# A hybrid attention layer on one core: loads a step earlier in the second half's preparation, the mask inside the scan, one small product on ScalarE

## The chip, the core and the metric

The kernel runs on one core of a Trainium2 chip. A core has TensorE (PE; its weight loads are listed apart as PEld), VectorE (DVE), ScalarE (ACT), GpSimd (POOL) and SyncE (SP), which in this kernel issues the transfers between HBM and the core's memory. Each engine takes its instructions in the order in which the program holds them for it; between engines they wait on semaphores. The metric is the device time of one execution in microseconds (us), the median of several.

## What is computed

One mixer layer with batch 1, sequence 2048 and width 1024, in float32:

```python
mod = c @ w_ada + b_ada
shift, scale, gate = split(mod, 3)
h = rmsnorm(x, norm_g) * (1 + scale) + shift
sb_q, sb_k, sb_v, sb_g, df_q, df_k, df_v, df_g = split(h @ w_in)
# group A, 8 heads of 64, stick-breaking, strictly causal (s < t):
#   A[t, s] = sigmoid(z_ts) * prod over s < j < t of (1 - sigmoid(z_tj))
# group B, 4 heads, two softmax maps of 64 and values of 128, ALiBi, causal
sb_out = stick_breaking(sb_q, sb_k, sb_v) * silu(sb_g)
df_out = rmsnorm(p1 @ v - lam * p2 @ v) * 0.8 * silu(df_g)
out = concat(sb_out, df_out) @ w_out
return x + gate * out
```

## The kernel before

The sequence is worked on in two halves of 1024 rows, each in two chunks of 512 columns. Matrix products keep near-float32 accuracy by splitting an operand into a rounded part and a rest (`wh` and `wl`, `hH` and `hL`, `aH` and `aL`) and adding three products (`mm3`, lines 381 to 383).

**Start (lines 1013 to 1026).** For each of the eight 128-row blocks of the width, DVE reduces two tiles of `w_ada` against `c` (`ada_block`, L179, two instructions of 512 columns for the scale and two for the shift). Then `gmul` = (1 + scale) times the norm's gain is made on DVE (L1015, a 128x1 instruction), ACT scales and shifts the transposed input with it (L310) and rounds it (L311), POOL or DVE forms the rest (L312), and PE runs twelve products.

**The second half's preparation (`prep_steps`, `ada_steps`).** The normalised input of the second half is made in small steps which are woven among the projections and the attention of the first half. For each chunk there are eight steps `one` that load a 128x512 block of `x`, square it on ACT (L220, L223) and add it on POOL (L224); one step that turns the sums into a factor; and eight steps `three` that load the block again (L253), scale it on DVE (L244) and on ACT (L335) and store it to HBM (L336). Then sixteen steps load a tile of `w_ada` (L198) and reduce it on DVE (L199) for the gate. Each step issues its load and uses it in the same step. The tiles come from a pool of eight buffers (`stage`), which the projections' outputs use too.

**Stick-breaking heads (`SBHead.front`).** A row block of 128 queries is cut into pieces of at most 512 columns, the rightmost piece first. Two matmuls per piece make the scores (L547). In the piece that holds the diagonal, a third matmul adds a 128x128 mask of -1e30 above and on the diagonal (L550, 128 in all: 8 heads with 16 row blocks each). ACT makes sigmoid(z) into `s` (L680) and sigmoid(-z) in place (L681); DVE runs a scan from right to left that multiplies sigmoid(-z) up into `u` (L684); POOL multiplies `s` by the shifted `u` (L688). In the rightmost piece the scan starts from 1.0:

```python
ps = scores(q, self.kch, i, c0, we, dg if 0 <= dg < w else None)
nc.scalar.activation(s[:, c0:c0 + w], ps[:, :w], AF.Sigmoid, scale=0.125)
nc.scalar.activation(ps[:, :w], ps[:, :w], AF.Sigmoid, scale=-0.125)
top = c0 + w == L
nc.vector.tensor_tensor_scan(out=u[:, c0:c0 + w][:, ::-1], data0=ur, data1=dist[:, :w],
                             initial=1.0 if top else u[:, c0 + w:c0 + w + 1],
                             op0=ALU.mult, op1=ALU.bypass)
```

`s` and `u` lie in a pool of six large buffers. Later PE transposes `s` (L583), ACT and DVE split it (L589, L590) and PE multiplies it with the values (L665, L666).

**What sets the order.** A planner lists attention steps and projection steps with costs and interleaves the two lists so that projections are done when a head needs them. A projection or preparation step may be issued only after an attention matmul some way back (`issue_after`). The framework then orders each engine's instructions by its own estimate of when they can run, so an edit in one place can move instructions elsewhere.

Of the kernel before, what the change touches and what calls it, by code (L numbers as in the profile page):

```python
# [8 lines left out]
F32R = mybir.dt.float32r  # L9
# [18 lines left out]
MASKED = -1e30  # L28
# [9 lines left out]
PREP0, PREP1 = -90, -90  # L38
POOL_H = (1, 2, 3, 4, 5, 6)
# [7 lines left out]
def build(ctx: ExitStack, tc, xT, xN, cT, cK, normg, w_adaT, b_ada, w_in, qg, kg, lam4, subg, w_out,  # L47
# [47 lines left out]
    dist = ctile([128, T], "dist")  # L95
    maskr = ctile([128, 128], "maskr", F32R)
# [6 lines left out]
    def more_constants():  # L103
# [6 lines left out]
        for h in range(NDF):  # L110
# [9 lines left out]
        mk = tmp0[:, 384:512]  # L120
        nc.gpsimd.memset(mk, 0.0)
        nc.gpsimd.affine_select(out=mk, in_=mk, pattern=[[-1, 128]], compare_op=ALU.is_gt,
                                fill=MASKED, base=0, channel_multiplier=1)
        nc.gpsimd.tensor_copy(maskr, mk)
# [58 lines left out]
    def ada_steps(third):  # L183
        st = {}

        def first():
            st["cb"] = [stage("cb") for _ in range(2)]
            for i in range(2):
                nc.sync.dma_start(st["cb"][i], cT[i * 512:i * 512 + 512].unsqueeze(0)
                                  .broadcast_to([128, 512]))  # L190

        def step(j, i):
            if i == 0:
                st["s"] = col.tile([128, 2], F32, name="adas", tag="adas", bufs=1)
            s = st["s"]
            r0 = third * 1024 + j * 128
            wt = stage("wada2")
            nc.sync.dma_start(wt, w_adaT[r0:r0 + 128, i * 512:i * 512 + 512])  # L198
# [119 lines left out]
    def prep_steps(ch):  # L318
        st = {}

        def one(k):
            xt = load_x(1, ch, k, stage("xt"))
            if k == 0:
                st["acc"] = stage("xacc")
            sq_add(st["acc"], k, xt)
# [4 lines left out]
        def three(k):  # L330
            if k == 0:
                st["rb"] = spread(st["y"])
            xt = load_x(1, ch, k, stage("xt"))
# [3 lines left out]
        return ([lambda k=k: one(k) for k in range(KT)] + [two, lambda: None, lambda: None]  # L337
# [205 lines left out]
    def scores(q, kch, i, k0, w, diag=None):  # L543
        ps = zps.tile([128, 512], F32, name="ps_z", tag="z")
        tl = slice((i % 2) * 128, (i % 2) * 128 + 128)
        for pt in range(2):
            last_pe[0] = nc.tensor.matmul(ps[:, :w], lhsT=q[:, pt, tl], rhs=kch[k0 // 512][:, :w],  # L547
                                          start=pt == 0, stop=pt == 1 and diag is None)
        if diag is not None:
            last_pe[0] = nc.tensor.matmul(ps[:, diag:diag + 128], lhsT=identr, rhs=maskr, start=False,  # L550
                                          stop=True)
# [95 lines left out]
    class SBHead(Head):  # L647
# [20 lines left out]
        def front(self, i, A):  # L668
# [3 lines left out]
            def step(c0, w, we, first):  # L672
# [5 lines left out]
                dg = i * 128 - c0  # L678
                ps = scores(q, self.kch, i, c0, we, dg if 0 <= dg < w else None)
                nc.scalar.activation(s[:, c0:c0 + w], ps[:, :w], AF.Sigmoid, scale=0.125)  # L680
                nc.scalar.activation(ps[:, :w], ps[:, :w], AF.Sigmoid, scale=-0.125)  # L681
                top = c0 + w == L
                ur = ps[:, :w][:, ::-1]
                nc.vector.tensor_tensor_scan(out=u[:, c0:c0 + w][:, ::-1], data0=ur, data1=dist[:, :w],  # L684
# [606 lines left out]
```

## Time and profile before

| what | value |
|---|---|
| time, median of 3 runs | 1735.38 us (1733.97 to 1741.11) |
| time of the profiled execution | 1733.63 us |
| its span, first to last instruction | 1731.8 us |
| busy: PE, PEld, DVE, ACT, POOL | 1669.4, 1494.2, 1236.3, 1000.3, 836.6 us |
| share of the span | 96%, 86%, 71%, 58%, 48% |
| PE matmuls | 10816 |
| moved by DMA | 268.15 MB, mean 155 GB/s |

Busy time counts an instruction from its start to its end; since matmuls are pipelined, one begins before the one ahead of it ends, and a busy PE need not be a PE at its peak. What one matmul really takes of PE's time is read from start to start.

### The profile page before, as it was taken

The page shows a single profiled execution, that of the slowest core. Times are in us where ns is not written, and L with a number is a line of the kernel's source. Part 1 is how long each engine was busy: PE and PEld are TensorE (multiplying, and loading weights), DVE is VectorE, ACT ScalarE, POOL GpSimd, SP SyncE. Part 2 cuts the span into 40 slices and gives each one's busy share as a digit, 9 for nine tenths or more (in the row PEclk, how much of TensorE's full clock was granted, in tenths as well). Part 3 has the DMA queues.
Part 4 walks back from the last instruction along what each step waited for, and adds up shares of the span by engine and source line. Part 5 has one row for each costly group of instructions (what it writes and reads, how often), then busy time and mean ns, then how long its engine had stood idle before and what let it go on. Part 6 is the DMA issues. An engine that isn't in the chain of part 4 may idle for free.

```text
span 1731.8 us, 31619 instructions
## 1 busy us (share of the span) xinstructions
PE 1669.4 (96%) x10816; PEld 1494.2 (86%) x10816; DVE 1236.3 (71%) x2556; ACT 1000.3 (58%) x2027; POOL 836.6 (48%) x1266
## 2 busy tenths in 40 slices
PE   7899899999999999999999999999999999999999
PEld 6688688899999889878898889899998978888887
DVE  6626455766566887767787887788788889888741
ACT  4625555456555454766776777687665645554521
POOL 3325455457545644655565465576332353223553
PEclk9999999999999999999999999999999999999999
DMA  9585767534654975434432332234433566443264
GB/s 348 167 236 162 199 201 240 184 108 117 200 169 142 286 211 163 149 107 117 128 116 89 102 98 86 80 104 126 132 99 108 164 208 200 128 134 129 88 220 149
DMA packets 212690, 268.15 MB, mean 155 GB/s; under 512 B 21424, under 2 KB 136368, under 8 KB 212400
## 3 DMA queue, kind: packets, MB, share of 16 engines
q1 hardware_dynamic: 212528, 266.12, 50.5%
q8 instruction: 86, 1.41, 0.3%
q14 instruction: 76, 0.62, 0.1%
HBM read 186.34 MB, written 79.69 MB: 154 GB/s over the span
## 4 chain that ended last, share of the span: by engine, by line
PE 64%; DVE 8%; DMA 4%; issue 4%; POOL 3%; ACT 3%; SPq 1%; DVEq 0%; ACTq 0%; POOLq 0%
PE ps_z L547 10%; PE ps_t L583 8%; PE ps_n L381 5%; PE ps_n L383 5%; PE ps_n L382 5%; PE ps_p L381 4%; PE ps_p L383 4%; PE ps_p L382 4%; PE av L666 3%; PE av L665 3%; PE ps_o L381 3%; PE ps_o L382 3%; PE ps_o L383 3%; DMA xt<-in_xT 2%; DVE u L684 1%
## 5 line engine op out<-in xcount | busy, mean ns | idle before, releaser
L688 POOL TENSOR_TENSOR s<-s,u 128x512 f32<-128x512 f32 (+4 forms) x320 | 306.2, 959 | 274.1 <-DVE u L684 238.5
L547 PE MATMUL ps_z<-kc,qc 128*128 128x512 f32 (+3 forms) x1280 | 358.8, 374 | 10.5 <-DVE u L684 7.9
L589 ACT CAST aH<-ps_t 128x512 fp32r<-128x512 f32 (+1 forms) x432 | 240.7, 567 | 168.7 <-PE ps_t L583 165.1
L590 DVE TENSOR_TENSOR aL<-ps_t,aH 128x512 fp32r<-128x512 f32 (+1 forms) x432 | 276.7, 650 | 79.7 <-ACT aH L589 78.3
L369 POOL TENSOR_TENSOR wl<-raw,wh 128x512 fp32r<-128x512 f32 x168 | 224.5, 1344 | 128.1 <-ACT wh L365 118.3
L381 PE MATMUL ps_n<-wh,hH 128*128 128x256 f32 x960 | 275.2, 287 | 2.5 <-DVE sl L392 2.2
L383 PE MATMUL ps_n<-wh,hL 128*128 128x256 f32 x960 | 271.6, 283 | 0.0
L382 PE MATMUL ps_n<-wl,hH 128*128 128x256 f32 x960 | 271.2, 283 | 0.4 <-POOL wl L369 0.4
L684 DVE TENSOR_TENSOR_SCAN u<-ps_z,u,dist 128x512 f32<-128x512 f32 x192 | 245.7, 1280 | 32.2 <-ACT ps_z L681 26.5
L780 ACT ACTIVATE e<-e,nm 128x1024 f32<-128x1024 f32 (+4 forms) x192 | 172.1, 898 | 125.3 <-DVE nm L778 121.0
L547 PEld LDWEIGHTS ps_z<-kc,qc 128*128 128x128 f32 x1280 | 210.8, 190 | 37.4 <-DVE u L684 13.4
L766 DVE CUSTOM_DVE_ANT_0 e<-ps_z,dist 128x512 f32<-128x512 f32 (+3 forms) x320 | 186.6, 604 | 50.8 <-PE ps_z L547 44.0
L680 ACT ACTIVATE s<-ps_z 128x512 f32<-128x512 f32 (+3 forms) x320 | 172.9, 540 | 77.4 <-PE ps_z L547 39.2
L381 PE MATMUL ps_p<-hH,wh 128*128 128x512 f32 x480 | 192.2, 406 | 6.1 <-ACT hH L311 6.1
L382 PE MATMUL ps_p<-hL,wh 128*128 128x512 f32 x480 | 190.5, 397 | 0.8 <-POOL hL L312 0.6
L383 PE MATMUL ps_p<-hH,wl 128*128 128x512 f32 x480 | 189.3, 394 | 0.0
L381 PEld LDWEIGHTS ps_n<-wh,hH 128*128 128x128 f32 x960 | 182.6, 191 | 7.0 <-DVE sl L392 2.5
L382 PEld LDWEIGHTS ps_n<-wl,hH 128*128 128x128 f32 x960 | 182.7, 191 | 3.7 <-POOL wl L369 0.6
L383 PEld LDWEIGHTS ps_n<-wh,hL 128*128 128x128 f32 x960 | 182.8, 191 | 1.8
L681 ACT ACTIVATE ps_z<-ps_z 128x512 f32<-128x512 f32 (+3 forms) x320 | 173.5, 542 | 0.0
L583 PE MATMUL ps_t<-ident,s 128*128 128x128 f32 x1088 | 168.6, 275 | 4.6 <-DVE aL L590 4.3
L665 PE MATMUL av<-aH,vc 128*128 128x256 f32 x576 | 160.7, 290 | 7.9 <-ACT aH L589 6.7
(190 smaller groups left out, 3456.0 us busy)
## 6 DMA issues: line engine op xcount, KB each, us to landing
qc<-qst SPq DMA_DIRECT2D x256, 128.0 KB, 3.1
raw<-in_w_in SPq DMA_DIRECT2D x120, 256.0 KB, 3.2
kc<-kst SPq DMA_DIRECT2D x96, 256.0 KB, 3.5
vc<-vst SPq DMA_DIRECT2D x48, 256.0 KB, 3.0
vc<-vdt SPq DMA_DIRECT2D x48, 256.0 KB, 3.6
raw<-in_w_out SPq DMA_DIRECT2D x48, 256.0 KB, 3.4
wada<-in_w_adaT SPq DMA_DIRECT2D x16, 512.0 KB, 8.3
qst<-sh SPq DMA_DIRECT2D x64, 128.0 KB, 2.5
```

What stands on the lines that cost most here:

```text
L369: (eng or nc.gpsimd).tensor_tensor(out=wl, in0=raw, in1=wh.bitcast(F32), op=ALU.subtract)
L381: nc.tensor.matmul(ps, lhsT=aH, rhs=bH, start=first, stop=False)
L382: nc.tensor.matmul(ps, lhsT=aH, rhs=bL, start=False, stop=False)
L383: nc.tensor.matmul(ps, lhsT=aL, rhs=bH, start=False, stop=last)
L547: last_pe[0] = nc.tensor.matmul(ps[:, :w], lhsT=q[:, pt, tl], rhs=kch[k0 // 512][:, :w], start=pt == 0, stop=pt == 1 and diag is None)
L583: nc.tensor.transpose(tp[:, pos * 256 + t * 128:pos * 256 + t * 128 + 128], A[t][0][:, sb * 128:sb * 128 + 128], ident)
L589: nc.scalar.copy(aH[:, f0:], tp[:, f0:])
L590: nc.vector.tensor_tensor(out=aL[:, f0:], in0=tp[:, f0:], in1=aH[:, f0:].bitcast(F32), op=ALU.subtract)
L665: nc.tensor.matmul(o, lhsT=v, rhs=aH, start=st, stop=False)
L684: nc.vector.tensor_tensor_scan(out=u[:, c0:c0 + w][:, ::-1], data0=ur, data1=dist[:, :w], initial=1.0 if top else u[:, c0 + w:c0 + w + 1], ...
L688: nc.gpsimd.tensor_tensor(out=s[:, c0:c0 + m], in0=s[:, c0:c0 + m], in1=u[:, c0 + 1:c0 + m + 1], op=ALU.mult)
L766: nc.vector.tensor_tensor_reduce(out=e[m][:, c0 + o:c0 + o + w], in0=ps[:, :w], in1=dist[:, d0:d0 + w], scale=1.0, scalar=-3e38, op0=ALU.a ...
```

## The change

Four edits.

- **Preload.** In `prep_steps` and `ada_steps` the load of a block is issued in the step before the one that uses it (`PRELOAD = 1`), and each phase gets a step of its own that issues its first load (57 steps in the place of 55).
- **Mask in the scan.** The mask matmul, the mask and its making on POOL are gone. The table `dist`, which is loaded once at the start, gets 128 more columns with a one on the diagonal. In the rightmost piece the scan starts from 0.0 and its second operation is a maximum against that table: right of the diagonal it stays 0, on it it becomes 1. In the other pieces it is as it was.
- **Last column.** In that piece ACT writes one column less of `s`, and POOL writes the last one with a memset of 128x1 (128 in all).
- **`gmul` on ACT.** The eight 128x1 products of the start are now ACT instructions (gain times scale plus gain).

```diff
@@ -92,8 +92,9 @@
-    dist = ctile([128, T], "dist")
-    maskr = ctile([128, 128], "maskr", F32R)
+    dist = ctile([128, T + 128], "dist")
...
@@ -117,11 +118,6 @@
-        mk = tmp0[:, 384:512]
-        nc.gpsimd.memset(mk, 0.0)
-        nc.gpsimd.affine_select(out=mk, in_=mk, pattern=[[-1, 128]], compare_op=ALU.is_gt,
-                                fill=MASKED, base=0, channel_multiplier=1)
-        nc.gpsimd.tensor_copy(maskr, mk)
@@ -188,14 +184,22 @@
             for i in range(2):
                 nc.sync.dma_start(st["cb"][i], cT[i * 512:i * 512 + 512].unsqueeze(0)
                                   .broadcast_to([128, 512]))
+            for n in range(PRELOAD):
+                ld(n)
+
+        def ld(n):
+            if n < 2 * KT:
+                j, i = n // 2, n % 2
+                r0 = third * 1024 + j * 128
+                wt = st[(j, i)] = stage("wada2")
+                nc.sync.dma_start(wt, w_adaT[r0:r0 + 128, i * 512:i * 512 + 512])
 
         def step(j, i):
+            ld(2 * j + i + PRELOAD)
             if i == 0:
                 st["s"] = col.tile([128, 2], F32, name="adas", tag="adas", bufs=1)
             s = st["s"]
-            r0 = third * 1024 + j * 128
-            wt = stage("wada2")
-            nc.sync.dma_start(wt, w_adaT[r0:r0 + 128, i * 512:i * 512 + 512])
+            wt = st.pop((j, i))
             nc.vector.tensor_tensor_reduce(out=wt, in0=wt, in1=st["cb"][i], scale=1.0, scalar=0.0,
                                            op0=ALU.mult, op1=ALU.add, accum_out=s[:, i:i + 1])
             if i == 1:
@@ -318,11 +322,16 @@
     def prep_steps(ch):
         st = {}
 
+        def ld(n):
+            if n < 2 * KT:
+                st[n] = load_x(1, ch, n % KT, stage("xt"))
+
         def one(k):
-            xt = load_x(1, ch, k, stage("xt"))
+            if k + PRELOAD < KT:
+                ld(k + PRELOAD)
             if k == 0:
                 st["acc"] = stage("xacc")
-            sq_add(st["acc"], k, xt)
+            sq_add(st["acc"], k, st.pop(k))
 
         def two():
             st["y"] = row_rstd(st["acc"])
@@ -330,11 +339,13 @@
         def three(k):
             if k == 0:
                 st["rb"] = spread(st["y"])
-            xt = load_x(1, ch, k, stage("xt"))
+            ld(KT + k + PRELOAD)
+            xt = st.pop(KT + k)
             scale_x(xt, k, st["rb"])
             nc.scalar.activation(xt, xt, AF.Identity, bias=mod[:, k:k + 1])
             nc.sync.dma_start(hst[k][ch], xt)
-        return ([lambda k=k: one(k) for k in range(KT)] + [two, lambda: None, lambda: None]
+        return ([lambda: [ld(n) for n in range(PRELOAD)]] + [lambda k=k: one(k) for k in range(KT)]
+                + [two, lambda: None, lambda: [ld(KT + n) for n in range(PRELOAD)]]
                 + [lambda k=k: three(k) for k in range(KT)])
 
     def fetch_steps(ch, hH, hL):
@@ -540,15 +551,12 @@
                               src[u % 2, :, :, qs:qs + 256].rearrange("l p t -> p l t"))
         return qt
 
-    def scores(q, kch, i, k0, w, diag=None):
+    def scores(q, kch, i, k0, w):
         ps = zps.tile([128, 512], F32, name="ps_z", tag="z")
         tl = slice((i % 2) * 128, (i % 2) * 128 + 128)
         for pt in range(2):
             last_pe[0] = nc.tensor.matmul(ps[:, :w], lhsT=q[:, pt, tl], rhs=kch[k0 // 512][:, :w],
-                                          start=pt == 0, stop=pt == 1 and diag is None)
-        if diag is not None:
-            last_pe[0] = nc.tensor.matmul(ps[:, diag:diag + 128], lhsT=identr, rhs=maskr, start=False,
-                                          stop=True)
+                                          start=pt == 0, stop=pt == 1)
         return ps
 
     def segs(n, ext):
@@ -675,16 +683,19 @@
                 if first:
                     tiles["u"], tiles["s"] = self.row("u", i), self.row("s", i)
                 u, s = tiles["u"], tiles["s"]
-                dg = i * 128 - c0
-                ps = scores(q, self.kch, i, c0, we, dg if 0 <= dg < w else None)
-                nc.scalar.activation(s[:, c0:c0 + w], ps[:, :w], AF.Sigmoid, scale=0.125)
+                ps = scores(q, self.kch, i, c0, we)
+                top = c0 + w == L
+                m = w - 1 if top else w
+                nc.scalar.activation(s[:, c0:c0 + m], ps[:, :m], AF.Sigmoid, scale=0.125)
+                if top:
+                    nc.gpsimd.memset(s[:, L - 1:L], 0.0)
                 nc.scalar.activation(ps[:, :w], ps[:, :w], AF.Sigmoid, scale=-0.125)
-                top = c0 + w == L
                 ur = ps[:, :w][:, ::-1]
-                nc.vector.tensor_tensor_scan(out=u[:, c0:c0 + w][:, ::-1], data0=ur, data1=dist[:, :w],
-                                             initial=1.0 if top else u[:, c0 + w:c0 + w + 1],
-                                             op0=ALU.mult, op1=ALU.bypass)
-                m = w - 1 if top else w
+
+                nc.vector.tensor_tensor_scan(out=u[:, c0:c0 + w][:, ::-1], data0=ur,
+                                             data1=dist[:, T + 128 - w:T + 128][:, ::-1] if top else dist[:, :w],
+                                             initial=0.0 if top else u[:, c0 + w:c0 + w + 1],
+                                             op0=ALU.mult, op1=ALU.max if top else ALU.bypass)
                 nc.gpsimd.tensor_tensor(out=s[:, c0:c0 + m], in0=s[:, c0:c0 + m],
                                         in1=u[:, c0 + 1:c0 + m + 1], op=ALU.mult)
 
@@ -1012,8 +1023,8 @@
     turn(xps[0], xn0, 0)
     for k in range(KT):
         after(rs0, lambda: ada_block(1, k, wa[(1, k)], cb))
-        nc.vector.scalar_tensor_tensor(out=gmul[:, k:k + 1], in0=mod[:, 8 + k:9 + k], scalar=1.0,
-                                       in1=ngt[:, k:k + 1], op0=ALU.add, op1=ALU.mult)
+        nc.scalar.activation(gmul[:, k:k + 1], mod[:, 8 + k:9 + k], AF.Identity,
+                             scale=ngt[:, k:k + 1], bias=ngt[:, k:k + 1])
         after(rs0, lambda: ada_block(0, k, wa[(0, k)], cb))
         make_h(k, 0, xps[k % 2], *hs[0], k in POOL_H)
         if k + 1 < KT:
@@ -1266,7 +1277,8 @@
         "subg": np.ascontiguousarray(a["subln_g"][0].reshape(128, 1)),
         "w_out": np.ascontiguousarray(a["w_out"][0]),
         "ident": np.eye(128, dtype=np.float32),
-        "dist": np.where(rel <= 0, rel, np.float32(-1e30)).astype(np.float32),
+        "dist": np.concatenate([np.where(rel <= 0, rel, np.float32(-1e30)),
+                                j[None, :128] == p[:, None]], axis=1).astype(np.float32),
     }
 
 
```

How it moves instructions. Two stretches of SP's queue stand here first; `xt` is a block of the input, `hst` the stored result of a step `three`, `qst`, `vst` and `gst` are other stores of the projections, `qc`, `vc`, `gt` and `raw` are loads. In the change line 257 is the load that was 253, and 346 the store that was 336.

SP, the first chunk's steps `three`, before:

```order
L336 DMA hst_0_197<-xt 128x512
L253 DMA xt<-in_xT 128x512
L336 DMA hst_0_199<-xt 128x512
L399 DMA qst_0_145<-sh 64x512 x2
L336 DMA hst_0_201<-xt 128x512
L399 DMA qst_0_145<-sl 64x512 x2
L253 DMA xt<-in_xT 128x512 x2
L709 DMA gt<-gst_0_163 64x512
L716 DMA mst_0_179<-ot 64x512
L399 DMA qst_0_143<-sh 64x512
L336 DMA hst_0_203<-xt 128x512
```

The same place in the change:

```order
L257 DMA xt<-in_xT 128x512
L346 DMA hst_0_196<-xt 128x512
L257 DMA xt<-in_xT 128x512
L346 DMA hst_0_198<-xt 128x512
L346 DMA hst_0_200<-xt 128x512
L410 DMA qst_0_144<-sh 64x512 x2
L410 DMA qst_0_144<-sl 64x512 x2
L257 DMA xt<-in_xT 128x512
L346 DMA hst_0_202<-xt 128x512
L257 DMA xt<-in_xT 128x512
L720 DMA gt<-gst_0_162 64x512
```

Two loads of these steps stand further up in both. The last number of a store counts its block in steps of two (197 or 196 is block 0). Before, the loads of blocks 3, 5 and 7 stand behind the store of the block ahead of them (here block 3, behind store 201); in the change each load stands ahead of the store of the block before its own.

SP, the second chunk's steps `three`, from the store of block 2 on, before:

```order
L336 DMA hst_1_202<-xt 128x512
L655 DMA vc<-vst_0_157 128x4x128 x2
L336 DMA hst_1_204<-xt 128x512
L655 DMA vc<-vst_0_157 128x4x128
L709 DMA gt<-gst_0_165 64x512
L655 DMA vc<-vst_0_157 128x4x128 x2
L362 DMA raw<-in_w_in 128x2x256
L253 DMA xt<-in_xT 128x512
L716 DMA mst_0_181<-ot 64x512
L436 DMA gst_0_167<-gt 128x512
L539 DMA qc<-qst_0_143 64x2x256 x2
L336 DMA hst_1_206<-xt 128x512
```

The same place in the change:

```order
L346 DMA hst_1_201<-xt 128x512
L663 DMA vc<-vst_0_156 128x4x128 x2
L373 DMA raw<-in_w_in 128x2x256
L550 DMA qc<-qst_0_142 64x2x256
L346 DMA hst_1_203<-xt 128x512
L373 DMA raw<-in_w_in 128x2x256
L720 DMA gt<-gst_0_164 64x512
L550 DMA qc<-qst_0_142 64x2x256
L663 DMA vc<-vst_0_156 128x4x128 x3
L257 DMA xt<-in_xT 128x512 x2
L447 DMA gst_0_166<-gt 128x512
L727 DMA mst_0_180<-ot 64x512
```

Here the loads of blocks 4 and 5 stand behind the store of block 3 in the change. Over the whole second chunk the loads of blocks 1, 4, 5 and 7 stood behind the store of the block ahead of them before, and those of blocks 4 and 7 do so in the change.

POOL, a place in the second half's stick-breaking heads (L688 and L699 are the product of `s` and `u`, 128x127 to 128x511 in the rightmost piece, L691 the new memset), before:

```order
L858 TENSOR_TENSOR ot<-ot,gt 128x512
L688 TENSOR_TENSOR s<-s,u 128x511
L688 TENSOR_TENSOR s<-s,u 128x512 x2
L714 TENSOR_TENSOR ot<-ot,gt 64x512
L688 TENSOR_TENSOR s<-s,u 128x512
L688 TENSOR_TENSOR s<-s,u 128x127
L688 TENSOR_TENSOR s<-s,u 128x512 x2
L688 TENSOR_TENSOR s<-s,u 128x255
```

The same place in the change:

```order
L869 TENSOR_TENSOR ot<-ot,gt 128x512
L691 MEMSET s 128x1 x2
L699 TENSOR_TENSOR s<-s,u 128x511
L699 TENSOR_TENSOR s<-s,u 128x512 x3
L725 TENSOR_TENSOR ot<-ot,gt 64x512
L699 TENSOR_TENSOR s<-s,u 128x127
L699 TENSOR_TENSOR s<-s,u 128x512 x2
L691 MEMSET s 128x1 x2
L699 TENSOR_TENSOR s<-s,u 128x255
```

The memsets of two row blocks stand together, ahead of the product of the first; the product of the second comes five to six rows later. On PE 128 instructions are gone, on DVE 8; on ACT the `gmul` of a block stands one to three rows ahead of the L310 that uses it.

## Rows read from the trace of the kernel before

**Rows 1.** The page's first part, whole span: busy us, share, instructions.

```profile
PE 1669.4 (96%) x10816; PEld 1494.2 (86%) x10816; DVE 1236.3 (71%) x2556; ACT 1000.3 (58%) x2027; POOL 836.6 (48%) x1266
```

**Rows 2.** Groups by line and shape, whole span: count, busy us, mean ns, idle before.

```profile
L590 DVE TENSOR_TENSOR aL<-ps_t,aH 128x512 fp32r<-128x512 f32 x336 | 225.4, 680 | 65.7 <-ACT aH L589 64.8
...
L688 POOL TENSOR_TENSOR s<-s,u 128x512 f32<-128x512 f32 x192 | 210.3, 1096 | 141.7 <-DVE u L684 123.3 <-DVE rs_y L147 7.8 <-ACT aH L589 1.8
...
L684 DVE TENSOR_TENSOR_SCAN u<-ps_z,dist 128x512 f32<-128x512 f32 x32 | 38.9, 1215 | 8.8 <-ACT ps_z L681 6.3 <-PE ps_t L583 2.4
...
L684 DVE TENSOR_TENSOR_SCAN u<-ps_z,dist 128x384 f32<-128x384 f32 x32 | 30.5, 952 | 4.0 <-ACT ps_z L681 2.5 <-POOL s L688 0.5
L550 PE MATMUL ps_z<-maskr,ident 128*128 128x128 f32 x128 | 30.4, 237 | 0.0
```

**Rows 3.** PE in order of time around one mask: start us, duration us, instruction.

```profile
232.53 0.56 PE L547 MATMUL ps_z<-kc,qc 128*128 128x384 f32 x2
232.93 0.22 PE L550 MATMUL ps_z<-maskr,ident 128*128 128x128 f32 x1
232.99 0.68 PE L547 MATMUL ps_z<-kc,qc 128*128 128x512 f32 x2
```

**Rows 4.** DVE in order of time in the start, three `gmul` and what follows.

```profile
22.27 0.16 DVE L1015 SCALAR_TENSOR_TENSOR gmul<-mod,ngt 128x1 f32<-128x1 f32 x1
...
25.50 1.29 DVE L1015 SCALAR_TENSOR_TENSOR gmul<-mod,ngt 128x1 f32<-128x1 f32 x1
...
29.87 1.29 DVE L1015 SCALAR_TENSOR_TENSOR gmul<-mod,ngt 128x1 f32<-128x1 f32 x1
31.08 0.73 DVE L179 CUSTOM_DVE_ANT_0 wada<-wada,ps_cb,badat 128x512 f32<-128x512 f32 x1
```

**Rows 5.** POOL in order of time in the same stretch.

```profile
29.86 1.28 POOL L312 TENSOR_TENSOR hL<-xh,hH 128x512 fp32r<-128x512 f32 x1 [0.58 <-ACT hH L311]
```

**Rows 6.** ACT in order of time in the same stretch.

```profile
32.71 0.78 ACT L310 ACTIVATE xh<-av,mod,gmul 128x512 f32<-128x512 f32 x1 [2.93 <-DVE mod L179]
```

**Rows 7.** PE in order of time in the same stretch, one block's products and the next block's transposes.

```profile
29.83 0.73 PE L381 MATMUL ps_p<-hH,wh 128*128 128x512 f32 x2
...
32.91 0.39 PE L383 MATMUL ps_k<-hH,kwl 128*128 128x512 f32 x1
33.54 0.66 PE L304 MATMUL av<-ident,xn 128*128 128x128 f32 x4 [0.24 <-ACT xh L310]
```

**Rows 8.** Stretches: us, then busy us and count of PE, PEld, DVE, ACT, POOL.

```profile
103.00:350.00 247.00, 229.04 (x1326) 196.99 (x1326) 138.37 (x204) 131.22 (x277) 120.78 (x142) 0.99 0.69 203
350.00:500.00 150.00, 150.00 (x1182) 145.73 (x1181) 93.74 (x188) 85.64 (x183) 84.34 (x140) 1.00 0.51 149
```

**Rows 9.** Who waited for whom on ACT, 103 to 350 us: us, times, longest.

```profile
ACT xsq L223 <- DMA xt<-in_xT: 25.0, 10, 6.4
...
ACT xacc L220 <- DMA xt<-in_xT: 9.7, 2, 5.8
```

**Rows 10.** The same on DVE.

```profile
DVE xt L244 <- DMA xt<-in_xT: 23.3, 11, 4.1
...
DVE wada L199 <- DMA wada<-in_w_adaT: 6.6, 6, 2.4
```

**Rows 11.** The chain of waits, 225 to 305 us: shares, then start us, us, what.

```profile
by line: DMA xt<-in_xT 35.1%; issue 9.2%; DMA wada<-in_w_adaT 6.7%; DMA raw<-in_w_in 5.6%; DVE xt L244 5.2%; DMA kc<-kst 5.1%; DVE u L684 4.5%; ACT xt L335 2.9%; ACT wh L365 2.9%; DMA vst<-stv 2.5%; SPq L655 2.3%; SPq L253 1.8%; SPq L336 1.
...
250.97 4.72 DMA xt<-in_xT
...
257.70 3.28 DMA xt<-in_xT
```

**Rows 12.** POOL's own memset of 128x1, durations min/median/max ns.

```profile
L1278 POOL MEMSET const-float32-0.0<- x1: 98/98/98, 0.2 to 0.2; 128x1 f32 x1
```

**Rows 13.** ACT's 128x2 instruction, its durations min/median/max ns.

```profile
L117 ACT ACTIVATE lexp<-ldot x1: 203/203/203, 74.9 to 74.9; 128x2 f32<-128x2 f32 x1
```

**Rows 14.** The load of the table `dist` (L1037), issued at 65.3 us.

```profile
DMA to landing us min/median/max: 6.5/6.5/6.5
```

More of the change, by code (lines that the diff above doesn't have):

```diff
@@ L27 @@
 NBIG = 6
-MASKED = -1e30
 NSTG = 8
@@ L38 @@
 PREP0, PREP1 = -90, -90
+PRELOAD = 1
 POOL_H = (1, 2, 3, 4, 5, 6)
```

## The prediction

> **What bounds the kernel now.** I read the page's first part first: PE is busy for 96% of the span, DVE for 71% [rows 1]. The reader should see PE as the engine that nearly always has work, and then distrust the number, because a matmul's busy time overlaps the next one's. So second the timeline, from start to start: the mask matmul of 128 columns starts at 232.93 and the next matmul at 232.99, 0.06 us later, though the groups give it a mean of 237 ns [rows 2, 3]. What an edit on PE is worth is counted in such steps. Third the stretches, to see where PE is not the bound: from 103 to 350 us PE is idle for 247.00 - 229.04 = 18.0 us, from 350 to 500 for nothing [rows 8]. Fourth the waits in that first stretch: ACT stands 25.0 + 9.7 us and DVE 23.3 + 6.6 us waiting for transfers of `xt` and `wada` [rows 9, 10]. Both take their instructions in order, so sigmoids, rounding and scans of the attention stand behind such a wait, and PE runs dry behind them. Last the chain of waits from 225 to 305 us: 35.1% of it is the landing of `xt` and 6.7% that of `wada`, 33 us of 80 [rows 11]. Two loads there start at 250.97 and 257.70: the store of one block waits on SP for ACT, and the next load stands behind that store.
>
> **The change part by part.** The sum is made against the profiled execution, 1733.6 us, of which 1731.8 are its span; the median of the runs shown, 1735.4, lies 1.8 us above it, so I add 1.8 at the end.
>
> *Mask matmuls removed.* 128 of them at 0.06 us from start to start [rows 3] are 7.7 us. They lie on PE's queue, and PE is the bound nearly everywhere outside the start and the preparation, so I count all: -7.7. The bounds are 0 (where PE waits anyway) and the busy time of the group, 30.4 us [rows 2], which I exclude as an end of the range because the steps overlap. The row shows 0.06 us per mask. [...]
>
> *`gmul` moved to ACT.* In the start DVE takes one block of the width in 29.87 - 25.50 = 4.37 us. `gmul` costs DVE 31.08 - 29.87 = 1.21 us while POOL works on L312 in the same microsecond, from 29.86 on, and lasts 0.16 us at 22.27, in a block without that row of POOL [rows 4, 5]. Six blocks have POOL's L312, so DVE loses at most 6 x 1.21 = 7.3 us of work. On ACT the nearest row is 0.20 us for 128x2 [rows 13], and ACT idles 2.93 us before its L310, waiting for DVE [rows 6]: eight such instructions hide there, and if that cover were gone they would cost 1.6 us. PE sets the next limit: its products of one block run from 29.83 to 32.91 and one step more, some 3.3 us, and the four transposes of the next block lie outside this [rows 7]. That leaves about 0.8 us per block of the 1.21: -5.0, bounds 0 and -7.3.
>
> *Loads a step earlier.* No work goes, only waits. The bound on one side is PE's whole idle time of the stretch, 18.0 us [rows 8]; on the other 0. The order of the change says how much: of the fourteen loads of steps `three` after the first of a chunk, seven stood behind the store of the block ahead (blocks 3, 5, 7 and blocks 1, 4, 5, 7), two still do (blocks 4 and 7 of the second chunk). Some of the waits of PE there belong to other transfers (`raw`, 5.6% of the chain, `kc`, 5.1%) [rows 11] and are the next to be late. I take somewhat more than half of the bound: -10. Each block is now held in one of the eight shared buffers for a step longer; the price of that, a load or an output that waits for a buffer, is what keeps me from taking five sevenths of 18.
>
> *Memset and the rest.* 128 memsets of 0.10 us [rows 12] are 12.5 us on POOL, which waits 123.3 us in total for the scan before the 128x512 products that follow them [rows 2]: hidden, unless the memset itself waits, which is a rival below. I put 0.5 us for it. One column less on ACT, three instructions fewer on POOL at the start and two empty steps more: nothing. The table `dist` grows by a sixteenth; its one load takes 6.5 us early in the program [rows 14]: nothing where it lands before the first piece of attention, and a sixteenth of 6.5, 0.4 us, where not. The scan keeps its length, its read of `dist` and its two operations: nothing, see the last rival.
>
> The sum: -7.7 - 5.0 - 10.0 + 0.5 = -22.2, that is 1711.4 for such an execution and 1713 for the median. Since nearly all instructions of the attention are ordered anew by the framework, I allow some 7 us either way for that (a third of the sum, my choice).
>
> **The rivals.**
>
> *The preload gains nothing.* The waits move from one transfer to the next: with the pool full, a load waits for its buffer, and SP stands still for it in order. For it speaks that two loads are still behind a store; against it the five that are not. Then -7.7 - 5.0 + 0.5 = -12.2, a median of 1723.
>
> *Everything hides.* All 18.0 us of PE's idle time in the preparation and 7.3 in the start go: -7.7 - 7.3 - 18.0 = -33.0, a median of 1702. Against it speak the other transfers in the chain.
>
> *The memset holds up POOL.* In the order the memsets of two row blocks stand together, ahead of the product of the first. The second writes a buffer that PE's transposes of an earlier row block must have left; if they have not, POOL stands, and the product behind it, its transposes and the values' matmuls are late. It decides from 22.7 / 128 = 0.18 us of delay on the path per memset on: then the gain is gone, and the median is 1735. Against it: POOL already stands and waits for the scan, 123.3 us over 192 products, 0.64 us for each [rows 2], and would spend that time waiting here.
>
> *The scan becomes slower.* The maximum might cost a step more per element than the bypass did. The scan takes (1215 - 952) / 128 = 2.05 ns per element [rows 2]; half of that more over the 128 rightmost scans, 32 x (128 + 256 + 384 + 512) = 40960 elements, is 42 us of DVE's time. If two thirds of it reached the path, 28 - 22.2 = +5.8, and all of it +20, a median of 1755. The price decides: only above 22 us on the path does it turn slower. No row of before shows a scan with two working operations. [...]
>
> **How the numbers follow.** The forecast (all of the first two terms, half or more of the third) gets 0.62, the useless preload 0.18, everything hidden 0.08, the memset 0.08, the slower scan 0.04. The likeliest gives 1713. Its own range, with 7 us for the new order, is 1706 to 1720; the useless preload and the full gain widen that to 1699 and 1729, which leaves out the memset rival, the slow scan and the tails. A measurement of this kernel can tell about 0.5%, 8.7 us, from no change: 1726.7. Faster than that are the forecast, full gain and most of the useless preload: 0.81. Within 0.5%: the rest of that rival, the memset and a part of the scan, 0.15. Slower: 0.04.
>
> **What would show it.** In the profile after: 10688 PE matmuls, no L550; the start's period of a block near 3.6 us where it was 4.37, and `gmul` on ACT at about 0.2 us; waits of ACT and DVE for `xt` between 100 and 350 us at less than half of the 64.6 us of [rows 9, 10], and PE's idle time there at about 8 us; the rightmost scans of 512 columns still at 1215 ns; POOL's memsets at 0.1 us with little wait ahead of them. The prediction is wrong if PE's idle time from 100 to 350 us stays near 18, if POOL's idle time ahead of the memsets grows to tens of microseconds, or if the scans lengthen.

## The result, and the profile after

The changed kernel takes 1711.8 us, the median of 4 runs (1711.0 to 1713.5); the kernel before took 1737.5 us beside it. The ratio is 0.9855, 95% interval 0.9835 to 0.9875: 25 us less, with 21.7 and 28.7 as the ends. Forecast were 1713 us and a range of 1699 to 1729. The total came out; of the three terms behind it, the mask came out far too large and the loads too small, and it was luck that these errors cancelled.

The profiled execution after took 1713.5 us. That of before, 1733.6, is one of the fastest of its kind: the medians of its kernel, taken four times for the runs below, are 1736.1 to 1737.5. So a distance read from two traces, 20.1 us here, comes out up to 5 us short of what the ratios give, and what is read below from this one trace of before carries that error.

The page's first part after, to be held against [rows 1]:

```profile
PE 1657.8 (97%) x10688; PEld 1482.0 (87%) x10688; DVE 1226.7 (72%) x2548; ACT 1004.3 (59%) x2035; POOL 845.2 (49%) x1391
```

The 128 masks are gone from PE's count and the eight `gmul` from DVE's, and POOL has the 128 memsets less three instructions. But PE's idle time (span less busy) only fell from 62.4 to 53.8 us, although the preparation alone gave more than that. The stretches of [rows 8], same columns, after:

```profile
103.00:350.00 247.00, 241.07 (x1400) 208.42 (x1398) 153.75 (x232) 145.37 (x303) 134.36 (x204) 0.99 0.72 212
350.00:500.00 150.00, 148.30 (x1185) 144.90 (x1183) 93.32 (x210) 84.54 (x179) 82.46 (x161) 0.99 0.50 145
```

In the first, PE's idle time fell from 18.0 to 5.9 us, and PE got through 1400 matmuls where it did 1326. In the second, where it idled for nothing, it now idles 1.7 us. The waits behind the first stretch, on ACT and then on DVE, as in [rows 9, 10]:

```profile
ACT xsq L227 <- DMA xt<-in_xT: 20.0, 7, 3.6
...
ACT xacc L224 <- DMA xt<-in_xT: 5.3, 1, 5.3
...
DVE xt L248 <- DMA xt<-in_xT: 16.7, 11, 5.9
DVE wada L203 <- DMA wada<-in_w_adaT: 14.7, 7, 5.6
```

These are 56.7 us where [rows 9, 10] have 64.6. The waits hardly shrank, PE's idle time fell to a third: here a wait of ACT or DVE costs time only where PE has no other work left. DVE waits longer for `wada` than before (14.7 against 6.6), and PE waits for nothing behind it.

The groups by shape after, against [rows 2, 12, 13]:

```profile
L695 DVE TENSOR_TENSOR_SCAN u<-ps_z,dist 128x512 f32<-128x512 f32 x32 | 39.0, 1217 | 12.0 <-ACT ps_z L692 11.8
L695 DVE TENSOR_TENSOR_SCAN u<-ps_z,dist 128x384 f32<-128x384 f32 x32 | 30.4, 951 | 8.2 <-POOL s L699 4.4 <-ACT ps_z L692 3.4 <-POOL xacc L228 0.3
...
L691 POOL MEMSET s<- 128x1 f32 x128 | 10.4, 99 | 34.1 <-PE ps_t L591 33.0
L1026 ACT ACTIVATE gmul<-mod,ngt 128x1 f32<-128x1 f32 x8 | 3.1, 386 | 2.5 <-DVE mod L175 2.2
```

The scan with a maximum takes 1217 and 951 ns where the one with a bypass took 1215 and 952: no step more. POOL does stand ahead of the memsets, 33 us of it for PE's transposes. `gmul` on ACT takes 386 ns, twice what I took from [rows 13].

Last, how far each kernel is from the kernel before at the same work, in us: the median over all of PE's matmuls of 25 us of before, each against its counterpart, from the traces. The single parts are told of below.

```
us in before   change  gmul  loads  mask   masks    masks   change with
                       alone alone  alone  left out doubled PRELOAD = 2
   50            -6.3   -5.9   0.1    0.8     1.0     0.5      -6.3
  100            -9.6   -6.3  -1.8   -0.5     0.7     0.8      -9.3
  225           -23.9   -5.7 -14.0    0.2    -1.8     3.3     -27.2
  425           -27.8   -5.4 -12.7   -3.3    -5.5     9.7     -34.2
  450           -23.6   -5.4 -12.7    0.0    -3.2    10.6     -30.9
  900           -27.5   -4.2 -13.4   -5.7    -5.2    12.4     -36.9
 1000           -23.6   -4.2 -13.5   -1.8     0.5    19.0     -33.3
 1375           -21.4   -5.6 -13.5   -1.5    -1.7    20.3     -32.4
 1600           -22.3   -6.7 -16.2  -1.5    -1.1    19.9     -33.7
 1725           -20.2   -4.6 -14.1    1.5     1.6    19.8     -33.0
```

The reader should see three things. `gmul` and the loads give what they give once, early, and it stays. The columns of the two kernels without mask matmuls gain while stick-breaking heads run (to 425 and to 900) and fall back behind them. And a step of 2 to 3 us stands between 1600 and the end in five of the seven columns, for parts that touch nothing there. That step goes with TensorE's granted clock, the third number from the end in these lines. The change, then the kernel before:

```profile
1625.00:1630.00 5.00, 3.62 (x14) 3.33 (x15) 4.97 (x6) 0.59 (x1) 4.93 (x6) 0.66 0.78 260
...
1600.00:1700.00 100.00, 98.07 (x525) 83.26 (x524) 55.81 (x122) 37.50 (x65) 54.61 (x70) 1.00 0.50 167
```

A mean of 0.66 over 5 us is some 3.4 us at half the clock, which by an estimate takes up to 1.7 us from PE: the trace of the change shows 0.50 from 1627 to 1629 us and 1.00 up to 1626 and from 1630 on, and its 128x512 matmuls start 0.43 us apart at 1629 us and 0.23 at 1630. Over 1500 to 1735 us the change and the other four columns with the step show 0.99; the kernel before and the two columns without the step show 1.00. Such places lie at other times too, and differently in each trace (0.98 over 200 to 300 us of the change, where before shows 1.00; 0.97 over 100 to 150 us of before, where the change shows 1.00), so a step of this size in the table need not come from an edit.

### The profile page after: what moved, and what is told of

Its sections match the earlier page's. It is cut to its first block, busy times and chain, and to the rows that moved or that the text cites. A ratio compares the mean times of both kernels' runs of the same rounds, so it can differ in the third digit from the quotient of the medians.

```text
span 1711.6 us, 31472 instructions
## 1 busy us (share of the span) xinstructions
PE 1657.8 (97%) x10688; PEld 1482.0 (87%) x10688; DVE 1226.7 (72%) x2548; ACT 1004.3 (59%) x2035; POOL 845.2 (49%) x1391
## 4 chain that ended last, share of the span: by engine, by line
PE 70%; DVE 10%; DMA 5%; ACT 4%; issue 4%; POOL 4%; SPq 1%; DVEq 0%; POOLq 0%; ACTq 0%
PE ps_z L558 11%; PE ps_t L591 8%; PE ps_n L392 6%; PE ps_n L394 6%; PE ps_n L393 6%; PE ps_p L392 4%; PE ps_p L393 4%; PE ps_p L394 4%; DVE u L695 3%; PE av L674 3%; PE ps_o L393 3%; PE ps_o L392 3%; PE ps_o L394 3%; PE av L673 3%; DMA xt<-in_xT 2%
## 5 line engine op out<-in xcount | busy, mean ns | idle before, releaser
L699 POOL TENSOR_TENSOR s<-s,u 128x512 f32<-128x512 f32 (+4 forms) x320 | 307.0, 961 | 246.8 <-DVE u L695 222.4
L689 ACT ACTIVATE s<-ps_z 128x512 f32<-128x512 f32 (+4 forms) x320 | 169.3, 541 | 67.9 <-PE ps_z L558 48.9
L692 ACT ACTIVATE ps_z<-ps_z 128x512 f32<-128x512 f32 (+3 forms) x320 | 168.5, 538 | 1.7
L376 ACT CAST wh<-raw 128x512 fp32r<-128x512 f32 x168 | 103.5, 622 | 105.8 <-PE ps_o L393 48.2
```

The lines of the kernel that those rows point to most:

```text
L699: nc.gpsimd.tensor_tensor(out=s[:, c0:c0 + m], in0=s[:, c0:c0 + m], in1=u[:, c0 + 1:c0 + m + 1], op=ALU.mult)
```

## The experiments

Each ran in five rounds beside the kernel before; the ratios are turned into us with 1737.

**One part at a time.** The theory, from the distances between the two traces at the same work (the expectations call these points milestones), was that the loads give more than I forecast and the mask nothing.

`gmul` alone:

```diff
-        nc.vector.scalar_tensor_tensor(out=gmul[:, k:k + 1], in0=mod[:, 8 + k:9 + k], scalar=1.0,
-                                       in1=ngt[:, k:k + 1], op0=ALU.add, op1=ALU.mult)
+        nc.scalar.activation(gmul[:, k:k + 1], mod[:, 8 + k:9 + k], AF.Identity,
+                             scale=ngt[:, k:k + 1], bias=ngt[:, k:k + 1])
```

> The kernel before with gmul alone on ACT. Theory (read from the milestones of the two traces: the first score matmul and the load of dist come 5.9 us earlier after the change): -6 us, about 1731, and nothing after the start changes it. Rival (the prediction's term): -5.0. A third way, that the gain of the start is swallowed by the waits for xt in the preparation: 0, and then the first load of xt is 6 us earlier but the last one is not.

Measured: 0.9958 [0.9945, 0.9972], -7.3 us (-9.6 to -4.9). In the traces 5.9 us are there at 50 us and stay, but for 1 to 2 us, to the end. The gain is real, and not swallowed; the interval just holds the predicted -5.0 as well.

The loads alone (the diff's parts in `ada_steps` and `prep_steps`):

> The kernel before with the loads a step earlier (x and modulation weights) and nothing else. Theory (milestones: between 101 and 400 us the distance to the kernel before grows from 5.9 to 26.5 us): the preload is worth about twice its predicted term, -18 to -20 us at 400 us and -14 to -20 at the end, 1718 to 1723. Rival (the prediction's term): -10, 1727. If it gains nothing: 1737.

Measured: 0.9899 [0.9884, 0.9914], -17.5 us (-20.2 to -14.9). The rival of a useless preload falls, and my -10 is outside the interval.

The mask alone (the diff's parts in `scores`, `SBHead.front` and the tables):

> The kernel before with the mask in the scan, the wider table and the memset, and nothing else. Theory (milestones: from 400 us to the end the distance does not grow by the masks' 6 us but shrinks from 26.5 to 20.2): the missing mask matmuls gain nothing that lasts, 0 to +5 us, 1737 to 1742. Rival (the prediction's term): -7.7 + 0.5, 1730, spread over both halves in proportion to the masks.

Measured: 0.9980 [0.9968, 0.9992], -3.5 us (-5.6 to -1.4). Neither: something lasts, but not the -7.2. Page, first part of this kernel (span 1733.3):

```profile
PE 1665.4 (96%) x10688; PEld 1483.5 (86%) x10688; DVE 1234.1 (71%) x2556; ACT 1002.9 (58%) x2027; POOL 846.8 (49%) x1391
```

PE is busy 4.0 us less than in [rows 1], and idle 67.9 us instead of 62.4: in these two traces PE waits for what it no longer computes. The sizes are rough, since busy time also carries the granted clock (a 128x512 matmul of the change is busy for 0.63 us at 0.50 and 0.39 at 1.00), 0.992 over this execution and 0.996 over that of before.

The change without the early loads (`PRELOAD = 0`):

> The changed kernel with PRELOAD = 0: each load in the step that uses it, gmul on ACT and the mask in the scan as in the change. Theory (preload worth 14 to 20 us, mask about nothing): 1726 to 1732. Rival (the prediction's terms, preload 10): 1722. PE's idle time from 103 to 350 us should be back near 18 us by both.

Measured: 0.9934 [0.9917, 0.9951], -11.5 us (-14.4 to -8.5), 1724.8 us, between the theory and the rival. The loads are worth 13 us on top of the other two parts, 17.5 alone. PE's idle time from 103 to 350 us is back at 247.00 - 230.40 = 16.6 us:

```profile
103.00:350.00 247.00, 230.40 (x1285) 194.21 (x1284) 143.47 (x211) 135.70 (x284) 121.39 (x191) 0.99 0.69 201
```

The parts alone add up to 28.3 us, the change is worth 25.2: within the intervals, no sign of a further effect.

**What a mask costs.** First the masks left out and nothing put in their place:

```diff
-                ps = scores(q, self.kch, i, c0, we, dg if 0 <= dg < w else None)
+                ps = scores(q, self.kch, i, c0, we)
```

> The kernel before with the 128 mask matmuls left out and nothing put in their place, so the diagonal blocks are not masked in this run: PE's share of the mask alone, without the memset, the wider table and the maximum in the scan. Theory (the gain of the masks is given back at the end of each stretch of stick-breaking heads, whatever replaces them): -1 to -4 us, as the mask alone (-3.1). Rival A (the memset on POOL eats the gain): -7 to -8 us here. Rival B (the predicted 0.06 us per mask is too high): -1 to -4 us too, but then the doubled mask costs less than 4 us.

Measured: 0.9984 [0.9970, 0.9998], -2.8 us (-5.2 to -0.3). So it is neither the memset nor the scan that eats the gain. Page, first part (span 1733.5):

```profile
PE 1660.8 (96%) x10688; PEld 1478.9 (85%) x10688; DVE 1235.7 (71%) x2556; ACT 998.3 (58%) x2027; POOL 836.3 (48%) x1266
```

8.6 us less busy, 10.3 us more idle than [rows 1] (72.7 against 62.4). This trace is 1.7 us longer than that of before, while the ratio says 2.8 us shorter; so 4 to 5 us of the balance belong to the one fast execution of before. Then each mask made twice:

```diff
-            last_pe[0] = nc.tensor.matmul(ps[:, diag:diag + 128], lhsT=identr, rhs=maskr, start=False,
-                                          stop=True)
+            for r in range(2):
+                last_pe[0] = nc.tensor.matmul(ps[:, diag:diag + 128], lhsT=identr, rhs=maskr, start=False,
+                                              stop=r == 1)
```

> The kernel before with each mask matmul made twice, 128 more matmuls of 128 columns. At 0.06 us each from start to start they are +7.7 us on PE. Theory (PE's queue is the bound in the stretches of the stick-breaking heads, but not at their ends): +3 to +8 us. Rival B (a mask costs less than its step of 0.06 us on the path): under +3 us.

Measured: 1.0089 [1.0075, 1.0104], +15.5 us (+13.0 to +18.1), about twice the upper end of the theory. PE in order of time at the first masks of this kernel:

```profile
234.02 0.56 PE L547 MATMUL ps_z<-kc,qc 128*128 128x384 f32 x2
234.42 0.33 PE L551 MATMUL ps_z<-maskr,ident 128*128 128x128 f32 x2
234.59 0.45 PE L547 MATMUL ps_z<-kc,qc 128*128 128x512 f32 x1
```

Two masks take 0.17 us from start to start where one took 0.06 [rows 3]: the second costs 0.11, and 128 of those are 14 us, nearly the whole +15.5. Rival B falls with that. The price is not that of a second mask alone. In before, a mask behind a piece of 128 columns costs nearly as much (897.58 to 897.68):

```profile
897.40 0.34 PE L547 MATMUL ps_z<-kc,qc 128*128 128x128 f32 x2
897.58 0.27 PE L550 MATMUL ps_z<-maskr,ident 128*128 128x128 f32 x1
897.68 0.34 PE L383 MATMUL ps_n<-wh,hL 128*128 128x256 f32 x1
```

Over all 128 masks of before, 89 take 0.06 us and 31 take 0.11, nearly all of these behind 128 columns; in the other eight PE's next matmul is late for another reason. All 128 come to an estimated 9.5 us, not 7.7. So the mask that was added cost about what its steps come to, and the one that was taken away gave back 2.8 of some 9.5.

Where the taken time goes is seen best from 880 to 1000 us of before, in the stick-breaking heads. The waits of PE there, before:

```profile
PE ps_t L583 <- DVE aL L590: 0.4, 2, 0.2
```

and in the changed kernel from 880 to 1000 us, which is some 25 us further on in the same heads:

```profile
PE ps_z L558 <- DVE u L695: 1.7, 4, 0.5
PE av L673 <- ACT aH L597: 0.5, 1, 0.5
PE ps_t L591 <- DVE aL L598: 0.3, 1, 0.3
```

PE had no wait worth the name; now it stands for the scan and for the rounding. One reading is that PE, with less to do, has caught up with DVE and ACT. The doubled masks show that this is not all. The same work with the masks left out, then with the masks doubled:

```profile
PE ps_z L547 <- DVE u L684: 2.1, 4, 0.7
PE av L665 <- ACT aH L589: 1.9, 1, 1.9
...
PE av L666 <- ACT aH L590: 1.9, 1, 1.9
PE ps_t L584 <- DVE aL L591: 0.7, 3, 0.3
PE ps_z L547 <- DVE u L685: 0.2, 1, 0.2
```

With more to do on PE, the wait of 1.9 us for the rounding is there all the same, for the same rounding: in both kernels ACT has it behind the sigmoids of the next pieces, before ahead of them. That is the new order. The wait for the scan, 2.1 us and 0.2, does go with PE having less to do. In the table the doubled kernel loses 6.6 us from 900 to 1000; of these its 12 second masks are an estimated 1.3 and a place at half the clock (its mean clock over 700 to 1000 us is 0.99, that of before 1.00) up to 1.7. The kernel without masks loses 5.7 there. So before has an order that is good at this place, and these edits of the masks give it up. How the missing 7 us divide between order and catching up stays open, and with it whether +15.5 against -2.8 says anything of adding and removing as such.

A second place is the end of the first heads, where ACT changes its table from the sigmoid to the exponential. The changed kernel, in order of time:

```profile
432.60 1.28 ACT L791 ACT_TABLE_LOAD   x1
...
433.09 0.51 PE L591 MATMUL ps_t<-ident,s 128*128 128x128 f32 x3
...
433.90 0.40 ACT L791 ACTIVATE e<-e,nm 128x128 f32<-128x128 f32 x1
...
434.30 0.57 ACT L597 CAST aH<-ps_t 128x512 fp32r<-128x512 f32 x1
...
434.92 0.39 PE L673 MATMUL av<-aH,vc 128*128 128x256 f32 x1 [1.32 <-ACT aH L597]
```

and ACT before, at the same place:

```profile
460.06 0.61 ACT L589 CAST aH<-ps_t 128x512 fp32r<-128x512 f32 x1
460.69 1.28 ACT L780 ACT_TABLE_LOAD   x1
```

Before, the rounding that PE needs next stands ahead of the load of the table, and PE waits for nothing; in the new order it stands behind it, and PE loses 1.7 us. The kernels with the mask alone and with the masks left out lose 1.7 and 1.5 us at this load too, the doubled one nothing. The other steps back in the table above were not taken apart one by one.

**The memset.** The change without it, ACT writing that column with the rest:

```diff
-                nc.scalar.activation(s[:, c0:c0 + m], ps[:, :m], AF.Sigmoid, scale=0.125)
-                if top:
-                    nc.gpsimd.memset(s[:, L - 1:L], 0.0)
+                nc.scalar.activation(s[:, c0:c0 + w], ps[:, :w], AF.Sigmoid, scale=0.125)
```

> The changed kernel without the memset: ACT writes the unused column with the rest, so the last column of s is not zero in this run. Theory (the memset's 33 us of waiting on POOL are hidden): within 2 us of the change, 1710 to 1714. Rival (the memset on POOL eats half of the mask's gain): -4 us against the change, 1706 to 1708.

Measured: 1711.7 us, 0.9863 [0.9849, 0.9877], against the change's 1711.8 and 0.9855. The 34 us ahead of the memsets are hidden; POOL's products wait for the scan anyway, 222.4 us in total in the change.

**Which loads.** `PRELOAD` split into three constants, in the kernel before with the loads' part of the diff, and one of them at 1 in each run (here that of steps `three`; then `one`, then the weights):

```diff
-PRELOAD = 1
+PRE_ONE, PRE_THREE, PRE_ADA = 0, 1, 0
```

> The kernel before with the loads a step earlier in steps three alone (the 16 blocks that are scaled and stored), the others in the step that uses them. Theory (the prediction's: a load that stood behind the store of the block ahead is what PE pays for): most of the 17.5 us that all preloads gave, -9 to -13, 1724 to 1728. Rival (a load in flight is what counts, wherever it stands, and both halves of the steps have 16 loads): -6 to -8, 1729 to 1731.

Measured: 0.9974 [0.9960, 0.9988], -4.5 us (-6.9 to -2.1). Below both, though the interval reaches the rival's -6.

> The kernel before with the loads a step earlier in steps one alone (the 16 blocks that are squared and summed). Theory (no store is in their way): -2 to -4, 1733 to 1735. Rival (every load in flight counts alike): -6 to -8, 1729 to 1731.

Measured: 0.9918 [0.9905, 0.9931], -14.2 us (-16.5 to -12.0). Above both: most of what all loads give (-17.5).

> The kernel before with the modulation weights alone a step earlier. Theory (in the traces of both preload runs DVE still waits 14 us for them, and PE waits for nothing there; the distance to the kernel before stands still from 300 us on): 0 to -2, 1735 to 1737. Rival (a third of the loads, a third of the gain): -5 to -6, 1731.

Measured: 0.9973 [0.9963, 0.9983], -4.7 us (-6.4 to -3.0), more than the theory and as much as `three`. It is not the early loads alone. With `PRE_ONE` at 0 the list of steps still begins with one empty step, so in both kernels the steps of the preparation come one place later in the plan. The kernel with the weights alone waits less in total for the `x` that it loads as before: ACT and DVE, 103 to 350 us,

```profile
ACT xsq L232 <- DMA xt<-in_xT: 30.9, 11, 5.9
...
DVE xt L253 <- DMA xt<-in_xT: 13.8, 7, 3.9
```

more on ACT and less on DVE than [rows 9, 10]. The empty step alone was not run, but the change with `PRELOAD = 0` has it too, and no early load: its -11.5 us are 0.7 more than `gmul` alone and the mask alone give together (-10.8). And if each of the three kernels held the same share of order, their sum of 23.4 us would count it three times where all loads together (-17.5) hold it once, which makes it 3 us. With intervals of 2 to 3 us on each number, how much of the two times 4.6 us is order stays open; these two sums speak for less than the whole. What is settled: the gain sits in steps `one`, which square and sum and have no store. PE's idle time of the stretch with `one` alone is 247.00 - 237.29 = 9.7 us:

```profile
103.00:350.00 247.00, 237.29 (x1386) 205.72 (x1385) 145.37 (x215) 136.12 (x289) 123.63 (x148) 0.99 0.70 206
```

**Further ahead.** `PRELOAD = 2`, then 3:

> The changed kernel with PRELOAD = 2: the loads go two steps ahead. Theory (after the change PE idles 5.9 us from 103 to 350 us, and that is all that an earlier load can still give): -5 to 0 us against the change, 1707 to 1712. Rival (the stage buffers run out, so that loads wait on SP for a buffer and block those behind them): 1714 to 1720.

Measured: 1701.2 us, 0.9805 [0.9791, 0.9818], -33.9 us (-36.3 to -31.6): 10.6 us under the change, and well beyond the 5.9 us of idle time that the theory took for all there was; the rival falls. In the table it gains 6.4 us on the change by 425 us, and 12.8 by the end; the rest comes piecemeal, where no load was moved. The two traces differ in their granted clock (0.998 against 0.994 over the execution), which by an estimate is worth up to 7 us of that column. The clock is not the gain itself: at 0.994 a run took 1701.5 us, those of the change 1711.0 to 1713.5. Beyond the 6.4 us, some 4 of the 10.6 stay unexplained. The reason for the first part shows in SP's queue and on ACT in the changed kernel, in order of time:

```profile
181.25 1.06 SPq L257 DMA_DIRECT2D xt<-in_xT  x2
...
187.98 0.62 ACT L227 ACTIVATE xsq<-xt 128x512 f32<-128x512 f32 x1
...
189.02 1.06 SPq L257 DMA_DIRECT2D xt<-in_xT  x2
...
192.39 0.63 ACT L227 ACTIVATE xsq<-xt 128x512 f32<-128x512 f32 x1 [3.42 <-DMA xt<-in_xT]
```

The planner sets two steps next to each other, so loads go out in pairs. One step ahead, the second step of a pair uses a load that went out with the pair itself, at 189.02, and ACT waits 3.42 us for it to land. Two steps ahead is a whole pair. With it, ACT's waits for `xt` in steps `one` fall from 20.0 + 5.3 to

```profile
ACT xacc L224 <- DMA xt<-in_xT: 4.8, 1, 4.8
ACT xsq L227 <- DMA xt<-in_xT: 2.9, 2, 2.3
```

and PE's idle time in the stretch from 5.9 to 247.00 - 244.13 = 2.9 us:

```profile
103.00:350.00 247.00, 244.13 (x1450) 214.09 (x1450) 158.05 (x238) 149.64 (x309) 136.73 (x209) 1.00 0.73 213
```

> The changed kernel with PRELOAD = 3. Theory (at 2 PE still idles 2.9 us from 103 to 350 us, all that is left): within 2 us of PRELOAD = 2, 1699 to 1703. Rival (three of eight stage buffers held by loads that are not yet used make later loads and outputs wait for a buffer): 1705 to 1715.

Measured: 1703.3 us, 0.9811 [0.9794, 0.9828]: the same as 2. The buffers hold, and a third step ahead gives no more.

## Why the prediction came out, point by point

*The bound.* Right for most of the program, and right that the preparation is the exception. Wrong in what I drew from it: that PE is the bound was taken to mean that time removed from PE is time won, whatever the new order does.

*Mask matmuls, -7.7.* This step failed. The size of a mask, 0.06 us, was read from one row and holds for 89 of the 128; with those at 0.11 us the term would have been some 9.5. And "I count all" does not hold: with the masks left out PE's busy time falls by 8.6 us and its idle time rises by 10.3 in the traces, and -2.8 us remain, -3.5 with the new scan. I named this end myself, "0 (where PE waits anyway)", and looked only for waits that were there before; the waits that came are new ones, for the scan, the rounding and behind a table load. The wait for the rounding comes with the new order, since doubling the masks brings it too. Neither size, 0.06 us or 0.11, told what removing the masks would bring.

*`gmul`, -5.0.* Right in mechanism, and short in size if anything: -7.3 us is my upper bound, but its interval (-9.6 to -4.9) still holds -5.0, and in the traces 5.9 us are there at 50 us. DVE in the start after:

```profile
24.13 0.75 DVE L175 CUSTOM_DVE_ANT_0 wada<-wada,ps_cb,badat 128x512 f32<-128x512 f32 x1
...
27.30 0.75 DVE L175 CUSTOM_DVE_ANT_0 wada<-wada,ps_cb,badat 128x512 f32<-128x512 f32 x1
```

A block takes 3.17 us where it took 4.37 [rows 4]. The whole 1.2 us are gone. The limit by PE that I set at some 3.6 us, from one block's products and the next one's transposes, is lower: the stretch of [rows 7] held waits. With them gone PE takes a block in 3.21 us, from one block's transposes to the next one's:

```profile
35.96 0.60 PE L308 MATMUL ps_x<-ident,xn 128*128 128x128 f32 x4
...
39.17 0.60 PE L308 MATMUL av<-ident,xn 128*128 128x128 f32 x4
```

`gmul` itself is longer than I took, and hidden: ACT still waits 0.42 us for DVE ahead of L314.

```profile
26.07 0.38 ACT L1026 ACTIVATE gmul<-mod,ngt 128x1 f32<-128x1 f32 x1
...
27.38 0.78 ACT L314 ACTIVATE xh<-ps_x,mod,gmul 128x512 f32<-128x512 f32 x1 [0.42 <-DVE mod L175]
```

The eight take 386 ns in the mean, with the gain as scale and as bias, both 128x1 operands; my nearest row, 203 ns, had neither. What makes the difference no run shows.

*Loads, -10.* Right in sign, short in size: -13 in the change, -17.5 (-20.2 to -14.9) alone. The reason I gave, "seven stood behind the store of the block ahead", fails. Those are steps `three`, and `three` alone gives 4.5 us at most; steps `one`, which have no store, give 14. What stood in ACT's queue was the landing time itself, 3.2 to 4.9 us for the twelve loads from 175 to 240 us of the changed kernel. And the sub-forecast that the waits would fall below half was wrong while PE's idle time, forecast at 8 and measured at 5.9, was right: waits of ACT and DVE were the wrong measure.

*Memset, +0.5; table, scan, 0.* Right, the memset for the reason given: POOL has to wait there anyway. But a sign that I had set for being wrong came all the same: POOL stands idle for 34.1 us ahead of the memsets, "tens of microseconds", and the time does not follow. The rivals of the memset and of the slower scan fall by the run without the memset and by the groups. The 0 for the scan in the sum was my estimate: no row of before shows a scan with two working operations. In the change it takes 1217 ns with the maximum, against 1215 with the bypass.

*The sum.* -22.2 forecast, -25.2 measured. The mask was some 4 us too much; `gmul` some 2, which its interval does not set apart from nothing, and the loads 3 or more too little. That these cancelled is luck. A range with 7 us for the new order held it, and the order does move single places by several us, as the stretch from 900 to 1000 us shows.

## What to carry to other kernels

On an engine that is busy 96% of the time, what is removed need not be won: before counting it, look at the engine just behind, at what stands in its queue where stages meet, and at what the framework does to the order. Make the same work twice as well as leaving it out: a place that loses time both ways has lost it to the order and not to the work. Price a short matmul by what stands ahead of it (0.06 or 0.11 us here), not by one row. A load one step ahead is not ahead at all when the planner issues steps in pairs (ACT waited 3.42 us for one here); count the distance in time, from the queue, and compare it with the landing time. Judge an early load by the bound engine's idle time, not by the waits of the engine that uses it.

## What the runs showed that I had not expected

A mask, a matmul of 128 columns, took 0.06 us behind a wider matmul and 0.11 behind another of 128, so adding a mask behind a mask does not price removing one. Taking 128 matmuls away gave back 2.8 us of some 9.5, and at the place where most is lost, doubling them loses as much. Single stretches of some 3.4 us at half the clock, at other times in each execution, by an estimate of up to 1.7 us each, make steps of some 2 us in a comparison of two traces. And two kernels that load different things early gave the same 4.6 us, of which the empty step that they share explains a part that stays open.
